# 42 instead of 68 early unit matrix matmuls, and narrow matmuls first in three of seven products

## The chip, the core and the metric

The kernel runs on one core of a Trainium2 chip. A core has a matmul engine (TensorE, PE in the profile, with its weight loads as PEld), VectorE (DVE), ScalarE (ACT), GpSimd (POOL) and SyncE (SP), which here issues DMAs. The metric is the device time of one execution in microseconds, as a median over several executions.

## What is computed

One layer of a hybrid encoder: the input, 512 tokens of width 2048 in float32, is normalised and projected by one large matrix. Its columns give four matrices (q, k, v and a gate) for each of three branches of four heads, and three merge gates of width 2048. Each branch is an attention of its own kind; the outputs are gated, projected up, weighted by the merge gates, summed, projected once more and added to the input.

```python
hn = rmsnorm(x, norm_g)
proj = jnp.einsum('bsd,dc->bsc', hn, w_in)
...
ya = forgetting_attention(qa, ka, to_heads(br[:, :, 0, 2]), f_logit)
yb = chunked_relpos_attention(qb, kb, to_heads(br[:, :, 1, 2]), rel_bias)
yc = stick_breaking_attention(to_heads(br[:, :, 2, 0]), to_heads(br[:, :, 2, 1]), to_heads(br[:, :, 2, 2]))
ys = jnp.stack([from_heads(ya), from_heads(yb), from_heads(yc)], axis=2)
ys = ys * jax.nn.silu(br[:, :, :, 3])
up = jnp.einsum('bsnw,nwd->bsnd', ys, w_up)
merged = jnp.sum(gates * up, axis=2)
return x + jnp.einsum('bsd,de->bse', merged, w_out)
```

## The kernel before

**Split numbers.** Every float32 operand is split into an upper part, rounded to a reduced float32 that TensorE multiplies in one pass, and a lower part, the rest (`split`, lines 242 to 251: ScalarE writes the upper part at L245, VectorE the lower at L249). A product is then upper x upper + upper x lower + lower x upper.

**Stages.** At the start TensorE runs `WARM` matmuls of a 128x128 unit matrix in bfloat16 (L403). Their result is never read. Then come:

- the first head: q, k, v and gate of branch C, head 0, side by side, as x arrives (`first_quad`; units 0 to 8). TensorE also multiplies by the forget gate's few columns (L1174), and a small matmul (L479) spreads the row norms, copied by ScalarE to `rstd` (L484). VectorE then scales the sixteen tiles of x (L500) and they are split again (L245, L249);
- four gate columns on the whole of x (`col_task`), units 9 to 16, in 512-column matmuls;
- from then on input columns by pairs, with Strassen's scheme in Winograd's form (`PairTask`): seven products instead of eight. There are 52 pairs: a gate pair beside the first head, three pairs for head (C,1), four for each of nine heads, four for the last head, (A,3), and at the very end, after the up projection, eight of the output projection.

**A unit.** A pair has seven units, one for each product p. A unit takes eight tiles j of 128x128 weights, as upper part `u.hi` and lower part `u.lo` (in the profile `wh` and `wl`, 128x1024 each). On each tile's upper part TensorE runs a matmul of 512 columns (upper and lower part of the input, side by side: the two halves of the bank), and on each tile's lower part one of 256 columns, onto the left half. All eight wide ones come first, then the eight narrow ones. The order of the products is (1, 2, 6, 5, 7, 3, 4), except in pairs called `late`. Products 6, 7 and 4 are summed onto the bank in which 1, and then 6 and 7, already lie (`more`), and 3 onto that of 5. Each waits for the copy of the bank's earlier sum (`self.ev[onto]`), and between the two stands a unit of another bank.

**Weights of a unit.** `prep` splits them two units ahead (`LA = 2`): three buffers of `wh` and of `wl` rotate. The lower part is awaited by `yield u.ready`, which stands between wide and narrow matmuls.

**The order of work.** A planner (`Flow`) runs while the program is written: it simulates TensorE, ScalarE and VectorE with fixed costs, and the order in which it starts instructions is the order in which they stand on each engine. Attention matmuls (scores, transposes, products with v) are slipped in between a unit's matmuls as they become ready. The unit matrix matmuls are no part of the plan.

Of the kernel before, what the change touches and what calls it, by code (L numbers as in the profile page):

```python
# [16 lines left out]
S = 512  # L17
D = 2048
HD = 128
NH = 4  # L20
# [5 lines left out]
UK = 8  # L26
NQ = 4
HS = S // 2
EPS = 1e-6
NEG = -1e30  # L30
WARM = 68
SCALE = HD ** -0.5
LA = 2

A, B, C = 0, 1, 2
Q, K, V, G = 0, 1, 2, 3
PE, ACT, DVE = 0, 1, 2
# [112 lines left out]
def mm_us(n, x=1):  # L150
    return x * max(0.115, n / 2400 + 0.0133)
# [11 lines left out]
def hybrid_kernel(  # L163
# [26 lines left out]
    def nm(s):  # L190
        uid[0] += 1
        return f"{s}_{uid[0]}"
# [12 lines left out]
    def acc(i=0):  # L205

        return pa.tile([P, S], F32, tag=f"acc{i}", name=nm("acc"), bufs=1 if i else 2)
# [10 lines left out]
    LH, RH = slice(0, HS), slice(HS, S)  # L218

    def two(ap):  # L220

        return ap.rearrange("p (h s) -> p h s", h=2)

    class Parts:


        def __init__(self, s, ev=None):
            self.t = xp.tile([P, 2, 2, HS], F32R, tag="x", name=nm(s))
            self.hi, self.lo = self.t[:, :, 0, :], self.t[:, :, 1, :]
            self.ev = ev or [Event(), Event()]  # L230
# [32 lines left out]
    def mm(ps, w, x, start=False, stop=False, more=False):  # L263
        nc.tensor.matmul(ps, w, x, start=start, stop=stop, skip_group_check=more)  # L264
# [70 lines left out]
    units = []  # L335
# [65 lines left out]
    nc.vector.memset(first_ps, 0.0)  # L401
    for _ in range(WARM):
        nc.tensor.matmul(first_ps[:, :P], identb, identb, start=True, stop=True)  # L403
# [137 lines left out]
    def strassen_ops(x1, x2, t23, t4):  # L541

        def part(ts, i):
            return lambda k: ts[k] and ts[k].both(i)

        return {1: part(x1, 0), 2: part(x2, 0), 3: part(x2, 1), 5: part(x1, 1), 6: part(t23, 0), 7: part(t23, 1),
                4: lambda k: t4[k // 2] and t4[k // 2].both(k % 2)}


    def halves(c):  # L550
        return [w_col[c, 0], w_col[c, 1]]
# [50 lines left out]
    class PairTask:  # L602
# [6 lines left out]

        def __init__(self, src1, src2, ops, c1_done=None, c2r_done=None, c2_done=None, late=False, rest=None):
            self.src, self.ops, self.late, self.rest = (*src1, *src2), ops, late, rest
            self.done = {"c1": c1_done, "c2r": c2r_done, "c2": c2_done}
            self.order = (1, 5, 2, 3, 6, 7, 4) if late else (1, 2, 6, 5, 7, 3, 4)
            self.w, self.there, self.ps = {}, {p: Event() for p in range(1, 8)}, {}
            self.ev = {p: Event() for p in range(1, 8)}
            self.units = [Pair(self, i) for i in range(7)]
# [36 lines left out]
        def mms_of(self, i):  # L655
            p = self.order[i]
            bank = (0, 1, 2, 0, 0, 1, 2)[i] if self.late else {2: 1, 5: 2, 3: 2}.get(p, 0)
            onto = None if self.late else {6: 1, 7: 6, 4: 7, 3: 5}.get(p)
            more = onto is not None
            self.bank = getattr(self, "bank", {})  # L660
            self.bank[p] = bank

            def go(u):
                if more:
                    yield self.ev[onto]
                    self.ps[p] = self.ps[onto]
                else:
                    yield accs[bank], 1
                    self.ps[p] = acc(bank)

                for j in range(UK):
                    yield lambda: self.ops[p](j) is not None
                    r, _, ev = self.ops[p](j)
                    yield ev
                    yield PE, mm_us(S)
                    mm(two(self.ps[p]), u.hi[:, j, :], r, j == 0 and not more, more=more)
                yield u.ready
                for j in range(UK):
                    yield PE, mm_us(HS)
                    mm(self.ps[p][:, LH], u.lo[:, j, :], self.ops[p](j)[1], stop=j == UK - 1, more=more)  # L680
            return go

        def after_of(self, i):
# [434 lines left out]
    def col(n, r, h):  # L1118
        return halves((n * 4 + r) * NH + h)

    def gate_col(n, d):
        return halves(NB * 4 * NH + n * DT + d)

    ops = strassen_ops(x1, x2, t23, t4)
    gates = [(n, d) for n in range(NB) for d in range(0, DT, 2)]

    def spill(n, d, c):
        gl[n, d] = dp.tile([P, S], F32, name=nm("gl"))
        nc.sync.dma_start(gl[n, d], c)
        stored(t2s, 1, 256)  # L1130

    def gate_units(late=False):
        n, d = gates.pop(0)

        def keep(i):
            def go(c):
                spill(n, d + i, c)
                return
                yield
            return go  # L1140
        units.extend(PairTask(gate_col(n, d), gate_col(n, d + 1), ops, keep(0), None, keep(1), late).units)

    def first_quad(head):

        ps = {}
# [79 lines left out]
    def schedule(head, a, b):  # L1225
        for (d, g), base in [(g, a) for g in head.stages()[0]] + [(g, b) for g in head.stages()[1]]:
            at(base + d, g)

    def first_head(n, h):
        hd = Head(n, h)  # L1230
        units.extend(first_quad(hd))

        cols = []
        for _ in range(2):
            g, d = gates.pop(0)
            cols += [(g, d), (g, d + 1)]
        t = [col_task(gate_col(*c), spilled(*c), b, used_g if i == 3 else None)
             for i, (c, b) in enumerate(zip(cols, (1, 2, 0, 0)))]
        for i in range(2):
            units.extend(u[i] for u in t)  # L1240
        at(OFF["fb"], forget_bias)
        gate_units(late=True)
        schedule(hd, OFF["a0"], OFF["b0"])

    def head(n, h, last=False):
        hd = Head(n, h, last)
        u0 = len(units)
        units.extend(PairTask(col(n, Q, h), col(n, K, h), ops, hd.got(Q), None, hd.got(K)).units)
        if not last and (n, h) != (C, 1):
            gate_units()  # L1250
        units.extend(PairTask(col(n, V, h), col(n, G, h), ops, hd.got(V), None, hd.got(G)).units)
        gate_units()
        if last:
            gate_units()
        schedule(hd, u0 + 7, u0 + 21)
        return hd

    first_head(C, 0)
    for n, h in [(C, 1), (C, 2), (C, 3)] + [(n, h) for n in (B, A) for h in range(NH)]:
        last_head = head(n, h, (n, h) == (A, NH - 1))  # L1260


# [307 lines left out]
```

## Time and profile before

| | us |
|---|---|
| median of 3 runs | 1339.41 |
| lowest and highest | 1338.91, 1339.82 |
| profiled execution, its own time | 1340.63 |
| span of that execution, first to last instruction | 1338.9 |
| TensorE busy in the span | 1324.5 |
| VectorE busy | 1113.1 |
| ScalarE busy | 793.0 |

A row of a timeline gives the start, the time to the end of the last of its instructions, the engine, the line of the kernel, the operation, what is written and read by the program's names, the shape and the count; in brackets stands the engine's idle time before it and what ended it. Ends of matmuls are modelled, so their pace is read from starts. A row of waits names the waiting engine and line, what it waited for, the sum, the number and the longest. A row of stretches gives the stretch, its length, busy time and count of the engine's instructions, the granted clock of TensorE, the share of DMA time and GB/s; a count includes instructions that run over the stretch's edge.

### The profile page before, as it was taken

What the parts mean: (1) busy time and instruction counts of PE and PEld (TensorE: products, weight loads), DVE (VectorE), ACT (ScalarE), POOL (GpSimd) and SP (SyncE); (2) the same over time, 40 slices, a digit from 0 to 9 for tenths busy, and PEclk for the clock granted to TensorE, in tenths of its full rate; (3) what the DMA queues carried; (4) which work ended last, traced back from release to release, by engine and by line L of the source; (5) the groups of instructions that cost most, each with busy time, mean ns of one, the idle gap of its engine ahead of it and who ended that gap; (6) DMA issues with size and microseconds to landing.
All of it is one profiled execution on the core that took longest, in us unless ns stands there. A gap on an engine that the chain in (4) does not pass through costs nothing.

```text
span 1338.9 us, 19796 instructions
## 1 busy us (share of the span) xinstructions
PE 1324.5 (99%) x7390; PEld 1148.3 (86%) x7390; DVE 1113.1 (83%) x1626; ACT 793.0 (59%) x1215; POOL 91.6 (7%) x115
## 2 busy tenths in 40 slices
PE   9999999999999999999999999999999999989998
PEld 7788888888888888888888888888888788878887
DVE  5899998888787887878888888878788877897786
ACT  7656665646566566665666556665577655444443
POOL 0000101000010000010000001000000000001000
PEclk9999999999999999999999999999999999989999
DMA  9457767677767777677877768777768655758883
GB/s 359 166 137 182 182 178 184 193 196 200 198 176 201 187 216 180 182 204 174 226 179 190 192 181 215 176 189 200 196 184 267 234 189 188 197 142 244 240 244 90
DMA packets 89824, 263.06 MB, mean 196 GB/s; under 512 B 10480, under 2 KB 12656, under 8 KB 89728
## 3 DMA queue, kind: packets, MB, share of 16 engines
q1 hardware_dynamic: 71152, 203.00, 45.5%
q0 software_dynamic: 14976, 54.53, 24.7%
q10 hardware_dynamic: 3600, 4.26, 0.9%
q8 instruction: 58, 0.95, 0.3%
q14 instruction: 38, 0.31, 0.1%
HBM read 242.06 MB, written 19.70 MB: 196 GB/s over the span
## 4 chain that ended last, share of the span: by engine, by line
PE 98%; DVE 1%; POOL 0%; issue 0%; ACT 0%; DVEq 0%; ACTq 0%; POOLq 0%
PE acc L264 84%; PE att L264 8%; PE att L986 1%; PE att L1090 1%; PE att L1089 1%; PE att L260 1%; PE att L261 1%; PE att L259 1%; PE att L1088 1%; PE att L403 0%; DVE wl L249 0%; PE att L1049 0%; PE att L1174 0%; PE att L890 0%; PE att L889 0%; DVE m L249 0%
## 5 line engine op out<-in xcount | busy, mean ns | idle before, releaser
L249 DVE TENSOR_TENSOR wl<-raw,wh 128x1024 fp32r<-128x1024 f32 (+2 forms) x413 | 493.9, 1196 | 145.2 <-ACT wh L245 141.8
L245 ACT ACTIVATE wh<-raw 128x1024 fp32r<-128x1024 f32 (+2 forms) x413 | 427.7, 1037 | 145.3 <-PE acc L264 62.8
L264 PE MATMUL acc<-x,wh 128*128 128x512 f32 x1600 | 415.4, 395 | 0.0
L264 PEld LDWEIGHTS acc<-x,wh 128*128 128x128 f32 x1600 | 285.8, 189 | 52.4 <-ACT x L245 2.6
L264 PE MATMUL acc<-t,wh 128*128 128x512 f32 x1056 | 271.7, 394 | 0.0
L264 PEld LDWEIGHTS acc<-x,wl 128*128 128x128 f32 x1504 | 210.4, 190 | 18.5 <-issue 0.5
L264 PE MATMUL acc<-x,wl 128*128 128x256 f32 (+1 forms) x1504 | 223.6, 289 | 0.0
L264 PEld LDWEIGHTS acc<-t,wh 128*128 128x128 f32 x1056 | 188.0, 189 | 32.1
L264 PEld LDWEIGHTS acc<-t,wl 128*128 128x128 f32 x1056 | 145.4, 190 | 11.1
L264 PE MATMUL acc<-t,wl 128*128 128x256 f32 x1056 | 149.2, 282 | 0.0
L280 POOL DMA_DIRECT2D raw<-in_w_col x88 | 76.1, 865 | 927.0 <-DMA raw<-in_w_col 572.5
L264 PE MATMUL acc<-m,wh 128*128 128x512 f32 x448 | 113.9, 396 | 6.3 <-DVE m L249 5.9
L264 PEld LDWEIGHTS acc<-m,wh 128*128 128x128 f32 x448 | 81.6, 191 | 21.6 <-DVE m L249 6.3
L756 ACT ACTIVATE c<-acc 128x256 f32<-128x256 f32 x50 | 19.1, 383 | 98.8 <-PE acc L264 93.8
L734 ACT ACTIVATE u<-acc 128x512 f32<-128x512 f32 x50 | 29.8, 596 | 64.9 <-PE acc L264 64.9
L264 PE MATMUL att<-y,wh 128*128 128x512 f32 x256 | 66.5, 390 | 1.3 <-DVE y L249 1.3
L264 PEld LDWEIGHTS acc<-m,wl 128*128 128x128 f32 x448 | 61.9, 193 | 5.1 <-DVE wl L249 0.8
L264 PE MATMUL acc<-m,wl 128*128 128x256 f32 x448 | 63.3, 285 | 0.4 <-DVE wl L249 0.4
L646 DVE TENSOR_TENSOR raw<-raw,raw 128x1024 f32<-128x1024 f32 x52 | 63.4, 1219 | 0.4
L640 DVE TENSOR_TENSOR raw<-raw,raw 128x1024 f32<-128x1024 f32 x52 | 63.4, 1218 | 0.4
L717 ACT ACTIVATE v<-acc 128x512 f32<-128x512 f32 x52 | 31.2, 599 | 50.3 <-PE acc L264 47.0
L264 PEld LDWEIGHTS att<-y,wh 128*128 128x128 f32 x256 | 47.9, 188 | 12.3 <-DVE y L249 2.4
(183 smaller groups left out, 1362.4 us busy)
## 6 DMA issues: line engine op xcount, KB each, us to landing
raw<-in_w_col SPq DMA_DIRECT2D x228, 512.0 KB, 4.5
raw<-in_w_col POOLq DMA_DIRECT2D x88, 512.0 KB, 6.4
raw<-in_w_out SPq DMA_DIRECT2D x40, 512.0 KB, 4.4
gl<-c SPq DMA_DIRECT2D x48, 256.0 KB, 2.7
raw<-in_w_up SPq DMA_DIRECT2D x32, 384.0 KB, 3.1
sg<-gl SPq DMA_DIRECT2D x48, 256.0 KB, 5.1
raw<-in_w_out POOLq DMA_DIRECT2D x16, 512.0 KB, 6.5
x<-in_xT SPq DMA_DIRECT2D x16, 256.0 KB, 6.1
```

Of the source, the lines that this page charges most:

```text
L245: nc.scalar.activation(hi, src, AF.Copy)
L249: nc.vector.tensor_sub(lo, src, f(hi))
L259: nc.tensor.matmul(ps, lh, rh, start=start, stop=False, skip_group_check=more)
L260: nc.tensor.matmul(ps, lh, rl, start=False, stop=False, skip_group_check=more)
L261: nc.tensor.matmul(ps, ll, rh, start=False, stop=stop, skip_group_check=more)
L264: nc.tensor.matmul(ps, w, x, start=start, stop=stop, skip_group_check=more)
L280: nc.gpsimd.dma_start(to, src, accum_op=ALU.add)
L640: nc.vector.tensor_add(w[1], w[1], w[5])
L646: nc.vector.tensor_add(w[2], w[2], w[1])
L717: nc.scalar.activation(self.v, ps, AF.Copy)
L734: nc.scalar.activation(self.u, ps, AF.Copy)
L756: nc.scalar.activation(c, ps[:, RH], AF.Copy, scale=-1.0)
```

## The change

`WARM` becomes 42. A flag `turns` is handed to the pairs; where it is set, products 6, 7 and 4 run their eight narrow matmuls first and the eight wide ones then. The flag is set for all pairs of the nine heads between (C,1) and (A,3), their gate pairs included: 36 pairs. The pairs of (C,1) and (A,3), the late ones and the output projection keep their order.

```diff
-WARM = 68
+WARM = 42
...
-                for j in range(UK):
-                    yield lambda: self.ops[p](j) is not None
-                    r, _, ev = self.ops[p](j)
-                    yield ev
-                    yield PE, mm_us(S)
-                    mm(two(self.ps[p]), u.hi[:, j, :], r, j == 0 and not more, more=more)
-                yield u.ready
-                for j in range(UK):
-                    yield PE, mm_us(HS)
-                    mm(self.ps[p][:, LH], u.lo[:, j, :], self.ops[p](j)[1], stop=j == UK - 1, more=more)
+                def wide(last):
+                    for j in range(UK):
+                        yield lambda: self.ops[p](j) is not None
+                        r, _, ev = self.ops[p](j)
+                        yield ev
+                        yield PE, mm_us(S)
+                        mm(two(self.ps[p]), u.hi[:, j, :], r, j == 0 and not more, last and j == UK - 1, more=more)
+
+                def narrow(last):
+                    yield u.ready
+                    for j in range(UK):
+                        yield lambda: self.ops[p](j) is not None
+                        _, r, ev = self.ops[p](j)
+                        yield ev
+                        yield PE, mm_us(HS)
+                        mm(self.ps[p][:, LH], u.lo[:, j, :], r, stop=last and j == UK - 1, more=more)
+                for step, last in ((narrow, False), (wide, True)) if p in (6, 7, 4) and self.turns else (
+                        (wide, False), (narrow, True)):
+                    yield from step(last)
...
     for n, h in [(C, 1), (C, 2), (C, 3)] + [(n, h) for n in (B, A) for h in range(NH)]:
+        turning[0] = (n, h) not in ((C, 1), (A, NH - 1))
         last_head = head(n, h, (n, h) == (A, NH - 1))
```

More of the change, by code (lines that the diff above doesn't have):

```diff
@@ L602, in hybrid_kernel, with __init__ @@
     class PairTask:
-        def __init__(self, src1, src2, ops, c1_done=None, c2r_done=None, c2_done=None, late=False, rest=None):
-            self.src, self.ops, self.late, self.rest = (*src1, *src2), ops, late, rest
+        def __init__(self, src1, src2, ops, c1_done=None, c2r_done=None, c2_done=None, late=False, rest=None, turns=False):
+            self.src, self.ops, self.late, self.rest, self.turns = (*src1, *src2), ops, late, rest, turns
             self.done = {"c1": c1_done, "c2r": c2r_done, "c2": c2_done}
@@ L1125, in hybrid_kernel @@
     gates = [(n, d) for n in range(NB) for d in range(0, DT, 2)]
+    turning = [False]
     def spill(n, d, c):
@@ L1140, in keep @@
             return go
-        units.extend(PairTask(gate_col(n, d), gate_col(n, d + 1), ops, keep(0), None, keep(1), late).units)
+        units.extend(PairTask(gate_col(n, d), gate_col(n, d + 1), ops, keep(0), None, keep(1), late,
+                              turns=turning[0]).units)
     def first_quad(head):
@@ L1247, in head @@
         u0 = len(units)
-        units.extend(PairTask(col(n, Q, h), col(n, K, h), ops, hd.got(Q), None, hd.got(K)).units)
+        units.extend(PairTask(col(n, Q, h), col(n, K, h), ops, hd.got(Q), None, hd.got(K), turns=turning[0]).units)
         if not last and (n, h) != (C, 1):
             gate_units()
-        units.extend(PairTask(col(n, V, h), col(n, G, h), ops, hd.got(V), None, hd.got(G)).units)
+        units.extend(PairTask(col(n, V, h), col(n, G, h), ops, hd.got(V), None, hd.got(G), turns=turning[0]).units)
         gate_units()
```

## The prediction

> **What bounds the kernel now.** I read the page's busy times, its chain of work, the waits of TensorE, and then TensorE's stretches.
>
> ```profile
> PE 1324.5 (99%) x7390; PEld 1148.3 (86%) x7390; DVE 1113.1 (83%) x1626; ACT 793.0 (59%) x1215; POOL 91.6 (7%) x115
> PE 98%; DVE 1%; POOL 0%; issue 0%; ACT 0%; DVEq 0%; ACTq 0%; POOLq 0%
> PE acc L264 <- DVE m L249: 5.9, 1, 5.9
> 58.00:1040.00 982.00, 982.00 (x5643) 1.00 0.72 191
> ```
>
> TensorE is busy 99% of the span, and the chain of waits is 98% TensorE. Its one large wait (5.9 us, third row) lies at the start of the output projection, which the change does not reorder. The last row is a stretch of 982 us: TensorE never stands idle in it, at full clock. All 36 reordered input pairs lie there. So time can be won in two ways only: start the dense stream earlier, or let the same matmuls follow each other more closely. It is lost if something new makes TensorE wait.
>
> **Part one: 26 fewer unit matrix matmuls.** The rows are the start of TensorE and of ScalarE, then TensorE's matmul counts in stretches.
>
> ```profile
> 2.12 6.48 PE L403 MATMUL att<-identb 128*128 128x128 bf16 x68 [2.12 <-DVE identb L312]
> 8.41 0.70 PE L264 MATMUL acc<-x,wh 128*128 128x512 f32 x2
> 4.58 0.72 ACT L419 ACTIVATE x<-x,small_in 128x512 fp32r<-128x512 f32 x1 [2.50 <-DMA x<-in_xT]
> 5.21 0.61 ACT L245 ACTIVATE wh<-raw 128x512 fp32r<-128x512 f32 x1
> 3.00:4.00 1.00, 1.00 (x12) 1.00 1.05 387
> 3.00:7.00 4.00, 4.00 (x41) 1.00 1.03 374
> 7.60:7.80 0.20, 0.20 (x7) 1.00 1.06 410
> 7.60:8.30 0.70, 0.70 (x16) 1.00 1.04 395
> ```
>
> The operands of the first real matmul are there at 5.21 + 0.61 = 5.82 us, yet it starts at 8.41, behind the 68 unit matmuls. Between 4 and 7 us there are 41 - 12 = 29 starts, about 105 ns each; between 7.8 and 8.3 us there are 9, or 55.6 ns. So the array runs at half pace first, and the pace doubles on the way. 68 matmuls in 8.41 - 2.12 = 6.29 us, n of them at 107 ns and the rest at 55.6, give n = 49: the change of pace is near 7.35 us. With 42, real work begins at 2.12 + 42 x 0.107 = 6.6 us, after the operands. If the pace still changes at 7.35, the first 0.75 us of real work does half of what it would do later, so its start is worth 6.6 + 0.37 = 6.97 us, 1.44 us earlier. That is 26 x 55.6 ns: wherever the change of pace falls between 6.6 and 8.4, the matmuls taken away are worth their fast price. The upper bound, with no slow start of the real ones, is 8.41 - 6.6 = 1.8 us; the lower is nothing, if what follows is late.
>
> What follows is the first stage, and there the nearest operand is the lower part of x tile 7 in the first gate column. The rows are of TensorE, ScalarE and VectorE.
>
> ```profile
> 37.24 1.02 PE L479 MATMUL att<-dg,tmpc 128*128 128x512 f32 x2
> 36.75 0.61 ACT L245 ACTIVATE x<-x 128x512 fp32r<-128x512 f32 x1
> 38.30 0.60 ACT L484 ACTIVATE rstd<-att 128x512 f32<-128x512 f32 x1 [0.93 <-PE att L479]
> 38.93 1.29 DVE L500 TENSOR_TENSOR x<-x,rstd 128x512 f32<-128x512 f32 x2 [0.22 <-ACT rstd L484]
> 40.49 1.22 DVE L249 TENSOR_TENSOR wl<-raw,wh 128x1024 fp32r<-128x1024 f32 x1 [0.26 <-ACT wh L245]
> 46.31 1.23 DVE L249 TENSOR_TENSOR wl<-raw,wh 128x1024 fp32r<-128x1024 f32 x1 [0.24 <-ACT wh L245]
> 57.65 3.94 PE L264 MATMUL acc<-x,wh 128*128 128x512 f32 x16
> 59.94 1.28 DVE L249 TENSOR_TENSOR x<-x,x 128x512 fp32r<-128x512 f32 x2
> ```
>
> TensorE takes two wide matmuls for each x tile from 57.65 on. The sixteenth, which reads x tile 7's lower part, starts at 61.2 us: the sixteen last 3.94 us, one alone 0.4 (its end is modelled), so the sixteenth starts 3.94 - 0.4 = 3.54 after the first. VectorE writes that part in the first half of the last row, done near 60.6: TensorE has 0.6 us of slack, and would want this tile 1.44 us earlier. VectorE is without a gap from 46.31 to that row, so it comes earlier only by the gaps ahead of it: 0.22, 0.26 and 0.24 us. These close, because ScalarE's copy of rstd waits 0.93 us for the matmul at 37.24; with TensorE earlier it starts when ScalarE is free, at 36.75 + 0.61 = 37.36. VectorE is then 0.72 us earlier, and TensorE can be 0.6 + 0.72 = 1.3 us earlier. I take 1.25; bounds 0.6 (no gap closes) and 1.44.
>
> **Part two: narrow matmuls first in products 6, 7 and 4.** No matmul, load, DMA or evacuation is added or removed; only the order within a unit turns. The order of a pair was, with W for eight 512-column matmuls and N for eight 256-column ones: 1 WN, 2 WN, 6 WN, 5 WN, 7 WN, 3 WN, 4 WN. It becomes 1 WN, 2 WN, 6 NW, 5 WN, 7 NW, 3 WN, 4 NW. Going round from 4 to the next 1, N is followed by W 7 times before and 4 times after, so each pair loses 3 steps of each kind. The question is what a step costs. The rows are TensorE's, of the gate columns, of undisturbed pair units, and of one place with a longer run of short matmuls.
>
> ```profile
> 63.24 3.79 PE L264 MATMUL acc<-x,wh 128*128 128x512 f32 x16
> 79.56 0.62 PE L264 MATMUL acc<-x,wh 128*128 128x512 f32 x2
> 125.56 2.00 PE L264 MATMUL acc<-x,wh 128*128 128x512 f32 x8
> 127.41 1.11 PE L264 MATMUL acc<-x,wl 128*128 128x256 f32 x8
> 147.91 0.40 PE L264 MATMUL acc<-t,wh 128*128 128x512 f32 x1
> 508.58 0.40 PE L264 MATMUL acc<-x,wl 128*128 128x256 f32 x2
> 509.06 2.00 PE L264 MATMUL acc<-t,wh 128*128 128x512 f32 x8
> 1025.72 0.29 PE L1088 MATMUL att<-ah,vh 128*128 128x256 f32 x1
> 1027.38 2.00 PE L264 MATMUL acc<-t,wh 128*128 128x512 f32 x8
> 1029.22 1.11 PE L264 MATMUL acc<-t,wl 128*128 128x256 f32 x8
> ```
>
> Wide matmuls among themselves: 63.24 to 79.56 is three gate units of 24, so 16.32 / 72 = 0.2267 us each, 1.813 for eight. Narrow ones among themselves: the fifth of a unit starts at 508.58, the next unit at 509.06, so 0.48 / 4 = 0.120 us each, 0.960 for eight. A unit would be 2.773 us. But eight whole units from 125.56 to 147.91 take 22.35, that is 2.794 each: a pair of steps costs 0.02 us. (The first W there takes 127.41 - 125.56 = 1.85: the cost sits in the wide matmuls after narrow ones.) It goes away only if sixteen narrow ones leave no more behind them than eight. The last three rows speak for that: six short matmuls and then a unit's eight narrow ones, 14 in all, run before 1027.38, and the wide eight after them take 1.84, as everywhere. So I count 3 x 36 x 0.0204 = 2.2 us. Bounds: 2.2, and a loss of 0.8, if the wide ones pay by the number of narrow ones before them and only the quicker start of N after W goes (some 7 ns, 108 times).
>
> The cover that goes: a turned unit needs its lower weights at its first matmul, where it had 1.84 us of wide ones in front. Each unit has one such row, so they are counted off against TensorE's; VectorE's row stands before the unit that it feeds.
>
> ```profile
> 504.88 1.22 DVE L249 TENSOR_TENSOR wl<-raw,wh 128x1024 fp32r<-128x1024 f32 x1
> 510.40 1.21 DVE L249 TENSOR_TENSOR wl<-raw,wh 128x1024 fp32r<-128x1024 f32 x1
> 515.10 0.86 PE L264 MATMUL acc<-t,wh 128*128 128x512 f32 x3
> 190.40 1.19 DVE L249 TENSOR_TENSOR wl<-raw,wh 128x1024 fp32r<-128x1024 f32 x1
> 192.39 2.00 PE L264 MATMUL acc<-t,wh 128*128 128x512 f32 x8
> 196.65 1.21 DVE L249 TENSOR_TENSOR wl<-raw,wh 128x1024 fp32r<-128x1024 f32 x1
> 197.98 2.00 PE L264 MATMUL acc<-t,wh 128*128 128x512 f32 x8
> ```
>
> Product 6 at 509.06 has its weights at 506.10, and product 7 at 515.10 at 511.61: 3.0 and 3.5 us to spare. The tightest place is the first turned pair, where stick-breaking scans fill VectorE: 0.8 us at 192.39 and 197.98 - 197.86 = 0.1 at product 7. With TensorE earlier there, some tenths may be waited. What waits is TensorE itself, and all matmuls behind it. The upper weights' buffer is also held 0.95 us longer, to the end of a turned unit; the order by hand places the split that reuses it after that end anyway. The bank waits do not change, since a whole unit lies between a product and the one added onto it. I take 0.2 us for new waits, bounds 0 and 1.
>
> Sum: -1.25 - 2.2 + 0.2 = -3.25 us. The profiled execution took 1340.63 us (span 1338.9), so 1337.4; the median of the runs is 1339.41, 1.2 lower, and there the sum gives **1336.2**.
>
> **The rivals.**
>
> (a) *The order is worth nothing.* Only the early start stays: -1.25, or 1338.2. The Trainium skill, "TensorE: Matmul & The Clock Gate", section "Back-to-back issue gap", gives the warm gap as N / 2.4 ns plus 2.5, with no word of the matmul before it, and by it turning the order would move nothing. Against it: 1.84 to 1.85 us for eight wide ones after narrow ones, 1.813 among wide ones. For it: a longer narrow run is shown at one place only.
>
> (b) *The early start is mostly used up.* TensorE arrives at x tile 7 and waits for VectorE, whose gaps do not close: 0.6 instead of 1.25, and a few tenths more in the first turned pair, so -2.2 - 0.6 + 0.3 = -2.5, or 1336.9. For it: VectorE's gapless rows from 46 to 60 us.
>
> (c) *Slower: turned units wait for their lower weights.* The place is the first matmul of each of 108 units, the price what VectorE is late. It decides from 3.45 / 108 = 32 ns a unit on; for a loss that can be told (0.2%, 2.7 us, is about what a measurement of this kernel tells from no change) it takes 57 ns, 6.2 us in all, or 1342.2. For it: VectorE is 83% busy, with 0.1 us to spare at 197.98. Against it: 3 us to spare elsewhere, so ten or more heads' worth of such places would be needed.
>
> (d) *It does not do what it says.* The flag is set ahead of each head and handed to its four pairs, so 9 x 4 = 36 pairs turn; products 3, added too, do not. I see no way past that, and give it no chance.
>
> **Chances and range.** The row is TensorE's, around the wait of 5.9 us.
>
> ```profile
> 1180.00:1188.00 8.00, 2.13 (x9) 0.81 0.60 145
> ```
>
> The granted clock is 0.81 on the mean there, so half for some 3 us. How long it stays low may change with where the wait falls in time; I allow 1 us either way. Forecast 0.58 (1335.2 to 1336.7 as its own range, that included), (a) 0.20, (b) 0.14, (c) 0.08. Faster by over 0.2% means below 1336.7: the forecast, 0.58. Within 0.2%: (a) and (b), 0.34. Slower: 0.08. The range reaches over the forecast, (b) and (a) with half a microsecond around them: 1334.8 to 1338.8.
>
> **What would show it.** The first real matmul near 6.6 us, and at 57.65 the same row about 1.3 us earlier; a step of TensorE's waits for VectorE's x near 59.5 us if (b). Runs of sixteen narrow and sixteen wide matmuls in the turned pairs: W16 near 16 x 0.2267 + 0.03 = 3.66 us if right, near 3.69 if the order is worth nothing. New rows "PE acc <- DVE wl" among the waits of TensorE would speak for (c). Wrong would be the whole if the 982 us stretch had idle time, or if the wait of 5.9 us grew as the work before it came earlier.

## The result

| | median, us | lowest and highest | executions |
|---|---|---|---|
| before | 1339.71 | 1338.89, 1341.13 | 20 |
| changed | 1337.01 | 1335.86, 1337.99 | 20 |

The ratio is 0.9977 (95% interval 0.9971 to 0.9983): 3.1 us less by the ratio, between 2.3 and 3.9; by the medians 2.7. The forecast was 3.25 us less and 1336.2 us. The profiled execution of the changed kernel took 1337.21 us (span 1335.5), 3.4 under the one of before.

The busy times on the page of the changed kernel:

```profile
PE 1321.0 (99%) x7364; PEld 1148.0 (86%) x7364; DVE 1112.6 (83%) x1626; ACT 791.0 (59%) x1215; POOL 91.7 (7%) x115
```

Two rows of its waits of TensorE (us in all, count, longest):

```profile
PE acc L264 <- DVE m L249: 5.9, 1, 5.9
PE acc L264 <- DVE wl L249: 0.4, 1, 0.4
```

TensorE in the stretch that answers to 58 to 1040 us of before (window, its length, busy time and count, granted clock, DMA share, GB/s):

```profile
56.60:1036.40 979.80, 979.80 (x5643) 1.00 0.72 192
```

The same 5643 matmuls, still without idle time, take 2.2 us less than 982.0. The wait of 5.9 us is as long as before, and the wait for `wl` is the one near the end that was there before. No new wait of the narrow matmuls shows among the waits. The start, in TensorE's timeline and then in VectorE's:

```profile
2.13 4.66 PE L403 MATMUL att<-identb 128*128 128x128 bf16 x42 [2.13 <-DVE identb L312]
6.55 1.15 PE L264 MATMUL acc<-x,wh 128*128 128x512 f32 x2
7.54 0.63 PE L264 MATMUL att<-x,wh 128*128 128x512 f32 x2
56.23 3.94 PE L264 MATMUL acc<-x,wh 128*128 128x512 f32 x16
```

```profile
59.18 1.29 DVE L249 TENSOR_TENSOR x<-x,x 128x512 fp32r<-128x512 f32 x2
```

Real work begins 1.86 us earlier, but its first two matmuls take 0.99 us instead of 0.54: they run at half clock. (The column for the granted clock reads 1.00 in such early rows too; the trace's record of it begins with its first change, to full, at 7.52 us here and at 7.43 in the profile of before. I say that the clock opens at that moment; ahead of it the pace shows the half clock.) At the first gate column 1.42 us of it are left (57.65 to 56.23), and the row of VectorE that the prediction took for x tile 7 comes 0.76 us earlier. Last, undisturbed turned units and the tightest place, in TensorE's timeline:

```profile
639.32 1.11 PE L264 MATMUL acc<-x,wl 128*128 128x256 f32 x8
640.27 1.12 PE L264 MATMUL acc<-t,wl 128*128 128x256 f32 x8
641.24 2.00 PE L264 MATMUL acc<-t,wh 128*128 128x512 f32 x8
643.08 1.98 PE L264 MATMUL acc<-x,wh 128*128 128x512 f32 x8
644.89 1.11 PE L264 MATMUL acc<-x,wl 128*128 128x256 f32 x8
...
195.59 1.11 PE L264 MATMUL acc<-x,wl 128*128 128x256 f32 x8
196.59 1.19 PE L264 MATMUL acc<-t,wl 128*128 128x256 f32 x8
197.62 1.33 PE L264 MATMUL acc<-t,wh 128*128 128x512 f32 x5
```

Sixteen narrow ones take 641.24 - 639.32 = 1.92 us, and the sixteen wide ones behind them 644.89 - 641.24 = 3.65: eight at 1.84, the next eight at 1.81. The extra time is paid once for a run of sixteen. At the tightest place, two runs of eight narrow ones take 197.62 - 195.59 = 2.03 instead of some 1.91: 0.12 us waited for the lower weights.

### The profile page after: what moved, and what is told of

It is laid out like the page before. It is cut to its first block, busy times and chain, and to the rows that moved or that the text cites. A ratio compares the mean times of both kernels' runs of the same rounds, so it can differ in the third digit from the quotient of the medians.

```text
span 1335.5 us, 19770 instructions
## 1 busy us (share of the span) xinstructions
PE 1321.0 (99%) x7364; PEld 1148.0 (86%) x7364; DVE 1112.6 (83%) x1626; ACT 791.0 (59%) x1215; POOL 91.7 (7%) x115
## 4 chain that ended last, share of the span: by engine, by line
PE 98%; DVE 1%; POOL 0%; issue 0%; ACT 0%; DVEq 0%; ACTq 0%; POOLq 0%
PE acc L264 84%; PE att L264 8%; PE att L995 1%; PE att L1098 1%; PE att L1099 1%; PE att L260 1%; PE att L261 1%; PE att L259 1%; PE att L1097 1%; DVE wl L249 0%; PE att L1058 0%; PE att L403 0%; PE att L1185 0%; PE att L899 0%; PE att L898 0%; DVE m L249 0%
## 5 line engine op out<-in xcount | busy, mean ns | idle before, releaser
L264 PEld LDWEIGHTS acc<-x,wh 128*128 128x128 f32 x1600 | 292.8, 188 | 58.9 <-ACT x L433 0.9
L264 PE MATMUL acc<-t,wh 128*128 128x512 f32 x1056 | 268.6, 393 | 0.0
L264 PE MATMUL acc<-t,wl 128*128 128x256 f32 x1056 | 152.7, 284 | 0.0
L264 PEld LDWEIGHTS acc<-t,wl 128*128 128x128 f32 x1056 | 139.6, 191 | 2.2
```

## The experiments

In each table, the starts of TensorE are those of the first real matmul, of the first matmul of 256 columns (the first pair), and of the first matmul of the up projection. The part between the last two holds all turned pairs; I call what a kernel saves in it the gain of the stream. Starts are those of each kernel's one profiled execution; leads are counted against the profile of before.

### One part alone

Two kernels: before with `WARM = 42`, and the change with `WARM = 68`.

```diff
-WARM = 68
+WARM = 42
```

> The kernel before with 42 unit matrix matmuls, order of the products as before. My theory, each matmul taken away is worth its fast price: 26 x 55.6 ns = 1.4 us faster. Rival, VectorE's tile 7 swallows half of it: 0.6 us faster. The two parts together measured 2.7 us; if they only add, the other part has the rest.

```diff
-WARM = 42
+WARM = 68
```

> The change with 68 unit matrix matmuls: the turned order alone. My theory, 108 steps from narrow to wide at 0.02 us: 2.1 us faster, the first real matmul at 8.4 us as before. Rival, the order is worth nothing: 0, and the whole change would be the early start. Sixteen wide matmuls in a row would then take 3.68 us and not 3.66.

| | median, us | ratio to before, interval | first real | first pair | up projection | lead at first pair | gain of the stream |
|---|---|---|---|---|---|---|---|
| before | | | 8.41 | 103.13 | 1038.50 | | |
| change | 1337.01 | 0.9977 (0.9971 to 0.9983) | 6.55 | 101.72 | 1034.99 | 1.41 | 2.10 |
| 42 alone | 1339.55 | 0.9996 (0.9987 to 1.0005) | 5.82 | 101.71 | 1037.09 | 1.42 | -0.01 |
| order alone | 1337.85 | 0.9983 (0.9974 to 0.9992) | 8.10 | 102.84 | 1036.11 | 0.29 | 2.10 |

The order alone is faster and gains 2.10 us in the stream, as in the change: rival (a) falls, and the two parts do not need each other. In the two profiles of the change and of before, 1.41 at the start and 2.10 in the stream, less 0.1 behind the late wait, make the whole difference of 3.4 us. The lead of 0.29 us of the order alone is none of its own: its clock opened earlier in that execution, at 6.77 us instead of 7.43.

The 42 alone cannot be told from no change by the times: its median is 0.56 us under that of the kernel before beside it (1340.11), near the rival's 0.6, and the interval of the ratio, from 1.7 us faster to 0.7 slower, leaves room for the theory's 1.4 as well. Its profile says why the lead is less than it could be. Here are TensorE at the start, TensorE further on, and ScalarE there:

```profile
3.70 2.31 PE L403 MATMUL att<-identb 128*128 128x128 bf16 x27
5.82 0.72 PE L264 MATMUL acc<-x,wh 128*128 128x512 f32 x2
```

```profile
34.27 0.61 PE L264 MATMUL att<-x,wl 128*128 128x512 f32 x2
35.74 1.10 PE L479 MATMUL att<-dg,tmpc 128*128 128x512 f32 x2 [0.86 <-ACT dg L475]
```

```profile
33.37 1.06 ACT L245 ACTIVATE wh<-raw 128x1024 fp32r<-128x1024 f32 x1 [1.40 <-DMA raw<-in_w_first]
34.34 1.26 ACT L475 ACTIVATE dg<-identf,small_n 128x128 f32<-128x128 f32 x4
```

In this execution the clock opened early, at 5.03 us, the unit matmuls were done at 5.8 us and the first real ones ran at once at full pace: 2.6 us ahead of the profile of before. At 35 us TensorE waits 0.86 us for the copies `dg`, which feed the norms' matmul (L479). They stand behind the split of unit 6's weights on ScalarE, and that waits 1.40 us for its DMA. Behind it 1.42 us of lead are left. The change has as much, but not for this reason. In its profile TensorE shows no wait at that place (ScalarE's row of the copies, then TensorE's):

```profile
34.29 1.27 ACT L475 ACTIVATE dg<-identf,small_n 128x128 f32<-128x128 f32 x4
35.83 1.02 PE L479 MATMUL att<-dg,tmpc 128*128 128x512 f32 x2
```

The copies end at 35.56 us, 0.27 before the matmul starts; where TensorE waits, it is some 0.15 (35.60 to 35.74 above). The change's lead is 1.41 from its third real matmul on: that is what its late clock left of it. So this matmul caps a lead that would be larger, and x tile 7, which I had named, does not. The cap is no fixed 1.4 us: it moves with the copies, and below it leaves 1.56 and 1.68 us in two other profiles.

### Other numbers of steps

The change with product 3 turned as well, and before with every unit of the 36 pairs in four runs of four.

```diff
-                for step, last in ((narrow, False), (wide, True)) if p in (6, 7, 4) and self.turns else (
+                for step, last in ((narrow, False), (wide, True)) if p in (6, 7, 4, 3) and self.turns else (
```

> The change with product 3 turned too: more turned units, but only 2 steps fewer in a pair than in the kernel before (5 of 7 stay), not 3. My theory, time follows the steps: 36 x 0.02 = 0.7 us slower than the change, so 2.0 us faster than the kernel before. Rival, each turned unit brings the gain for itself (its weights or its bank come better): 36 more of them are 0.7 us faster than the change, 3.4 us faster than before.

```diff
+                a, b = range(UK // 2), range(UK // 2, UK)
+                if self.turns:
+                    for step, js, last in ((wide, a, False), (narrow, a, False), (wide, b, False), (narrow, b, True)):
+                        yield from step(last, js)
+                else:
+                    yield from wide(False)
+                    yield from narrow(True)
```

> The kernel before, with four wide, four narrow, four wide, four narrow matmuls in every unit of the 36 pairs: 252 steps from narrow to wide more. My theory, each step has its price whatever the length of the narrow run: about 252 x 0.02 = 5 us slower, at least 4, since a run of four ends before the fifth slow wide matmul. Rival, the wide ones pay by the number of narrow ones before them: no change. Rival, order is worth nothing: no change.

| | median, us | ratio to before, interval | first pair | up projection | gain of the stream |
|---|---|---|---|---|---|
| four products turned | 1337.51 | 0.9979 (0.9970 to 0.9988) | 101.45 | 1035.04 | 1.78 |
| runs of four | 1342.41 | 1.0018 (1.0009 to 1.0027) | 102.91 | 1040.22 | -1.94 |

More turned units gain less (1.78 against 2.10), so the gain is no gift to each turned unit; by steps it should have been 1.4 to 1.5. Counted in the traces, attention matmuls included, a 512-column matmul follows a shorter one 409 times before, 276 times in the change and 295 times here. By that count the gains stand in the same proportion: 2.10 us for 133 steps fewer, 1.78 for 114, 16 ns each. That the attention matmuls, which fall into other places, bring the difference is therefore likely; no run tests it. Splitting a unit loses time, which neither rival allows, but 1.9 us and not 4 to 5. Its timeline of TensorE, two undisturbed units:

```profile
623.25 1.09 PE L264 MATMUL acc<-t,wh 128*128 128x512 f32 x4
624.18 0.63 PE L264 MATMUL acc<-t,wl 128*128 128x256 f32 x4
624.65 1.09 PE L264 MATMUL acc<-t,wh 128*128 128x512 f32 x4
625.58 0.64 PE L264 MATMUL acc<-t,wl 128*128 128x256 f32 x4
626.06 1.09 PE L264 MATMUL acc<-x,wh 128*128 128x512 f32 x4
```

A unit takes 2.81 us (623.25 to 626.06) against 2.79 of before. Four wide ones take 0.93 where 0.907 is their price among themselves: each run pays nearly the whole extra. But the narrow runs are shorter too, 0.47 and 0.48, so a second step in a unit costs some 0.013 us net, not 0.020. That would be 3.3 us for 252 units; where the other 1.4 went I did not settle. The count in the trace, 643 steps and so 234 more than before, does not account for it.

### The wait of 5.9 us and the clock

The times of one kernel spread over some 2 us, nearly as much as the effect. TensorE's row for 1184 to 1192 us, just behind the wait, in the profile of before:

```profile
1184.00:1192.00 8.00, 4.81 (x16) 0.57 0.86 198
```

The granted clock is 0.57 of full there. In each of the eight profiles without filling the wait is 5.9 us, and the half clock lasts 6.83 us; but only 3.0 (order alone) to 5.9 us (runs of four) of it fall on work, the rest on the wait. So 100 unit matmuls, never read, were put into the wait, in the kernel before and in the changed one:

```diff
+                        if self.rest is not None and self.late and p == 6 and j == UK - 1:
+                            yield atts, 1
+                            ps = att()
+                            for _ in range(FILL):
+                                nc.tensor.matmul(ps[:, :P], identb, identb, start=True, stop=True)
+                            give(atts)
                         yield ev
                         yield PE, mm_us(S)
```

> The kernel before, with 100 unit matrix matmuls (never read) put where TensorE waits 5.9 us at the start of the output projection, in product 6 of the first output pair, ahead of its last wide matmul. They fill 5.6 us of that wait. My theory: the spread of the kernel's times (1338.8 to 1341.1) is mostly the half clock after this wait, whose length (3.0 to 5.9 us in the profiles so far) hangs on the phase of the clock's windows; with the wait filled the half clock does not come, the median falls by about 2.0 us to 1338 and the granted clock shows no 0.5 near 1185 us. Rival, the clock has no part in it: the same time, or up to 0.5 us slower where a filled matmul delays the first real one.

> The changed kernel with the same 100 matmuls in the same wait. My theory: 1335.0 us median with a spread under 1 us, so 2.9 to 3.1 us under the filled kernel before: with one of the two sources of spread gone, the change shows its stream gain of 2.1 us and an early start of 0.8 to 1.0 us. Rival, the early start is worth 1.4 us in every execution: 3.5 us under the filled kernel before. Rival, it is worth nothing on the mean: 2.1 us under it.

Later the two parts were run alone with this filling.

> The kernel before with the late wait filled (that alone: 1338.2 us) and with 42 unit matrix matmuls; the order of the products as before. My theory, an early start of 1.4 us in executions whose clock opens late and less where it opens early, since TensorE then meets the norms' matmul: 0.8 to 1.0 us under the filled kernel before on the median, 1337.3, and a spread of about 0.5 us instead of 1.6. Rival, 26 x 55.6 ns in every execution: 1.4 us, 1336.7, and the same spread.

> The kernel before with the late wait filled and the turned order, 68 unit matrix matmuls. My theory, 2.1 us under the filled kernel before in every execution: 1336.1, with its spread of about 1.6 us. Rival, the order's gain depends on the early start: less than 1.5 us.

| wait filled | median, us | lowest and highest | executions | ratio to the kernel before, interval |
|---|---|---|---|---|
| before | 1338.16 | 1337.28, 1338.85 | 11 | 0.9989 (0.9981 to 0.9998) |
| 42 alone | 1336.93 | 1336.74, 1337.38 | 11 | 0.9978 (0.9969 to 0.9987) |
| order alone | 1335.87 | 1335.33, 1336.40 | 7 | 0.9971 (0.9960 to 0.9981) |
| change | 1335.14 | 1334.84, 1335.32 | 5 | 0.9967 (0.9955 to 0.9980) |

TensorE in the filled kernel before, the same eight microseconds:

```profile
1184.00:1192.00 8.00, 7.74 (x86) 1.00 0.86 214
```

The half clock is gone, the median falls by 1.4 to 1.5 us (2.0 were expected), and the spread of before by 0.7 us, from 2.2 to 1.6; that of the change falls from 2.1 to 0.5, in five executions. So the clock behind the wait made part of the spread, and of the kernel before not the larger part, as the theory had it. What is left of it in the filled kernel before, 1.6 us, goes with the start: with 42 unit matmuls it shrinks to 0.6. The profiles, ordered by the moment at which the clock opens, show how:

| unit matmuls | profile of | clock opens, us | lead at first pair, us |
|---|---|---|---|
| 68 | wait filled, before | 8.13 | -0.36 |
| 68 | before | 7.43 | 0 |
| 68 | runs of four | 6.93 | 0.22 |
| 68 | order alone | 6.77 | 0.29 |
| 68 | wait filled, order alone | 5.91 | 0.69 |
| 42 | wait filled, 42 alone | 7.80 | 1.26 |
| 42 | change | 7.52 | 1.41 |
| 42 | four products turned | 6.72 | 1.68 |
| 42 | wait filled, change | 5.28 | 1.56 |
| 42 | 42 alone | 5.03 | 1.42 |

With 68, the lead grows by nearly half of what the clock opens earlier, over a range of 1.05 us. With 42 it grows as well down to 6.72 us and is smaller for the two that open earlier still: they have more at first (2.5 and 2.6 us) and lose it to operands. That is the cap at work, and it has a second place, which took 0.5 us from the filled change, a wait for a part of x:

```profile
12.81 0.73 PE L265 MATMUL acc<-x,wh 128*128 128x512 f32 x2 [0.24 <-ACT x L246]
```

The change is worth 3.0 us between filled kernels, the order 2.3, and 42 for 68 between 0.7 (with the order turned) and 1.2 (without, where the theory had 0.8 to 1.0 and the rival 1.4). The order alone spreads over 1.1 us, not 1.6. These differences cross two sets of executions on different occasions, and by the ratios each has an interval of more than 1 us; the medians fit the account of the profiles and do not prove it.

### Fewer unit matmuls still

The change with `WARM = 16`.

```diff
-WARM = 42
+WARM = 16
```

> The changed kernel with 16 unit matrix matmuls; they end near 3.9 us, and TensorE stands idle until the first operands at 5.8 us. Theory, the clock opens only after a window of about 3.4 us that is mostly busy, so the idle time puts the opening off: real matmuls at half pace until 8 to 11 us, and about 1 us slower than the change, though the first real matmul is earlier. Rival, only the place of the first real matmul counts: the same as the change, since it already runs into the wait for the norms' matmul, or faster by up to 0.5 us.

It took 1337.70 us (ratio to before 0.9985, interval 0.9976 to 0.9994), 0.7 over the change, which the intervals do not tell apart. Its timeline of TensorE does:

```profile
2.12 1.89 PE L403 MATMUL att<-identb 128*128 128x128 bf16 x16 [2.12 <-DVE identb L312]
5.83 1.22 PE L264 MATMUL acc<-x,wh 128*128 128x512 f32 x2 [1.82 <-ACT wh L245]
8.55 1.06 PE L264 MATMUL att<-x,wh 128*128 128x512 f32 x2
9.40 1.06 PE L264 MATMUL acc<-x,wl 128*128 128x512 f32 x2
10.26 0.79 PE L264 MATMUL att<-x,wl 128*128 128x512 f32 x2
10.89 0.62 PE L264 MATMUL acc<-x,wh 128*128 128x512 f32 x2
```

Real work begins at 5.83 as it should, and runs two matmuls in 0.85 us (8.55 to 9.40), half pace, until after 10.3 us; the record has full clock from 10.62 on. At the first pair (102.81) only 0.32 us of the lead of 2.58 are left. In none of the thirteen other profiles does the clock open later than 8.13 us, so the idle 1.82 us put its opening off; this is one execution.

### Lifting the cap

ScalarE's copies for the norms' matmul go ahead of the weights of unit 6 (the edit holds back units 6 to 8), alone, with the wait filled, and with 35 unit matmuls besides.

```diff
         yield u.source_there()
+        if u in units[6:9]:
+            yield dg_ev
         yield from split(u.hi, u.lo, u.source(), n, u.ready, hi_ev=u.ready_hi)
...
             nc.scalar.activation(dg[:, blk(b)], identf, AF.Copy, scale=y[:, b:b + 1])
+        set_(dg_ev)
```

> The changed kernel with ScalarE's order turned at one place: the four copies that feed the norms' small matmul go ahead of the split of the weights of unit 6, which waits for its DMA. Theory, what caps the early start is that matmul (in the run with 42 unit matmuls alone TensorE waited 0.9 us for it and gave back 1.1 us of a 2.5 us lead): the wait of TensorE for ScalarE's copies goes, executions whose clock opens early keep their lead, and the median falls by 0.3 to 0.5 us against the change. Rival, the lower part of x tile 7 caps it just as well: no change, and TensorE then waits for VectorE near 59 us.

> The changed kernel with the late wait filled (that alone: 1335.1 us, spread 0.5) and ScalarE's copies for the norms' matmul put ahead of the weights of unit 6. My theory, the cap of the early start was that matmul: the lowest times fall to about 1333.8, the median by 0.4 to 0.8 us, and the spread grows to over 1 us. Rival, x tile 7 caps it just as well: the same median and spread.

> As the one before, with 35 unit matrix matmuls, which end near 5.9 us, when the first operands are there. Theory, without the cap each matmul taken away is worth up to 55.6 ns: 7 of them 0.3 to 0.4 us. Rival, something else in the first stage caps: no change against the one before.

| | median, us | lowest and highest | executions | ratio to before, interval |
|---|---|---|---|---|
| copies first | 1336.87 | 1335.87, 1338.53 | 11 | 0.9980 (0.9971 to 0.9989) |
| wait filled, copies first | 1334.95 | 1334.56, 1335.42 | 5 | 0.9964 (0.9951 to 0.9976) |
| the same with 35 | 1334.48 | 1334.29, 1334.73 | 5 | 0.9960 (0.9947 to 0.9972) |

The first two are inconclusive: 0.1 and 0.2 us under the kernels without it, less than the theories' 0.3 to 0.8, and the profiled executions of both had a late clock (7.79 and 7.99 us), so that no cap was met. In the third the clock opened at 6.97 us. This is its timeline, of TensorE and then of ScalarE (the edits shift the line numbers: L483 here is L479 of the kernel before):

```profile
34.28 1.02 PE L483 MATMUL att<-dg,tmpc 128*128 128x512 f32 x2
37.46 0.61 PE L265 MATMUL att<-x,wh 128*128 128x512 f32 x2
38.05 0.73 PE L265 MATMUL acc<-x,wh 128*128 128x512 f32 x2
```

```profile
35.93 1.06 ACT L246 ACTIVATE wh<-raw 128x1024 fp32r<-128x1024 f32 x1 [1.31 <-DMA raw<-in_w_first]
36.90 0.58 ACT L488 ACTIVATE rstd<-att 128x512 f32<-128x512 f32 x1
37.38 0.62 ACT L246 ACTIVATE x<-x 128x512 fp32r<-128x512 f32 x1
```

The norms' matmul starts at 34.28 without a wait (it stands four matmuls earlier in TensorE's order here), and the lead of 2.0 us is the same ahead of it and behind it. The next thing caps: at 38.05 TensorE is late by some tenths (0.59 us between two starts instead of 0.45), for a part of x that ScalarE writes from 37.38 on, behind a split that waited 1.31 us for its DMA. 1.75 us of lead are left at the first pair (101.38), against 1.68 at most with the copies in their old place. With the first stage's loads as they are, another cap follows closely. This version, 1334.48 us, is the fastest of all, 5.4 us under the kernel before by the ratio.

The same profile settles x tile 7. TensorE at the end of the first gate unit, then VectorE:

```profile
59.22 0.62 PE L265 MATMUL acc<-x,wh 128*128 128x512 f32 x2
59.67 0.62 PE L265 MATMUL acc<-x,wl 128*128 128x512 f32 x2
59.30 1.28 DVE L250 TENSOR_TENSOR x<-x,x 128x512 fp32r<-128x512 f32 x2
```

All sixteen wide matmuls have started before 59.67 us, without a wait, while the first half of VectorE's row ends only after 59.9. So that row does not write what they read.

## The prediction, step by step

- **What bounds it.** Right. The stretch has no idle time after the change either, and the gain came from an earlier start and a closer sequence. The wait of 5.9 us stayed 5.9. The half clock behind it was misread: "half for some 3 us" is what the row from 1180 to 1188 us holds, and it goes on to 1191.9, 6.83 us in all. No term of the sum hangs on it, only the 1 us either way in the range.
- **26 unit matmuls at their fast price, 1.44 us.** Right for an execution whose clock opens as late as in the profile of before: 1.41 at the first pair, with the two real matmuls at half pace that the sum allowed for. That the clock of the changed kernel's profile opened at nearly the same moment (7.52 against 7.43 us) is luck; in the other profiles it opens anywhere from 5.0 to 8.1, or 10.6 with 16 unit matmuls.
- **The cap, 1.25 us.** The working is wrong, and that the profile shows 1.41 is luck: it is the 1.44 of the term above, with no cap met. I named x tile 7. VectorE's gaps closed as I said (0.76 us instead of 0.72), but the row at 59.94 that I took for the tile writes others (the profile with 35 shows it). Counted in order, it holds tiles 8 and 9, which TensorE reads from unit 13 on, and tile 7 is the row at 55.81, done 4.7 us before its matmul: nothing was near there. What caps the lead, where the clock opens early, is the norms' matmul, whose row I had quoted: I read it only as what releases VectorE, not as a wait of TensorE itself, and did not set its operand's end against it. And the profile is one draw: where the clock opens early, the kernel before has part of the lead already and the change gains less. Over many executions the early start was worth 0.7 to 1.2 us, by the filled kernels.
- **108 steps at 0.02 us, 2.2 us, less 0.2 for new waits.** Right: 2.10 in the stream, in the change and alone, with 0.12 us waited at the place that was named, product 7 near 196 us. In the traces a unit's wide matmul stands directly behind a narrow one 108 times less, and 2.10 + 0.12 us over 108 is 0.0206 us a step. Wide runs of sixteen took 3.65, as forecast for a price that does not grow with the narrow run. That the price is fixed for any length is not so: with runs of four a further step cost about two thirds in undisturbed units, and less on the whole.
- **(a)** falls by the order alone and by the runs of four. The Trainium skill's formula in "TensorE: Matmul & The Clock Gate", section "Back-to-back issue gap", knows nothing of the matmul before; here the same matmuls in another order took 2.10 us less, and the measurement decides.
- **(b)** was nearer in time than the forecast: the median, 1337.01 us, lies 0.1 from its 1336.9, and outside the forecast's own range (1335.2 to 1336.7). By the difference, the 2.7 us of the medians are nearer to its 2.5 than to the forecast's 3.25, the 3.1 of the ratio nearer to the forecast. Its mechanism, a wait at x tile 7, was not there; an early start used up by an operand was seen in a run, at another instruction.
- **(c)** had its price once, 0.12 us, instead of 108 times.

The shortfall of the median against the forecast is 0.8 us in time and 0.55 in difference: 0.3 of the 0.8 is the kernel before, whose median is 1339.71 here and was 1339.41 ahead of the prediction. The 3.25 us lie within the interval of the ratio. The early start, which hangs on the clock's phase, is the term that the runs make smaller.

## What to carry to other kernels

Where a profile is one execution and a clock's phase differs between executions, ask of each microsecond won at the start whether every execution has it to win, and look for the first operand that arrives on a time of its own: a fixed arrival turns an earlier start into a wait. A row that releases another engine is also an instruction with operands of its own; set them against it. In a dense stream of matmuls the order of two widths is worth reading from the starts, and merging runs cost next to nothing here, 0.12 us at one place, since the operands mostly lay ready far ahead.

## What the runs showed of the hardware

- Eight matmuls of 512 columns behind narrower ones take 1.84 us instead of 1.81, and the extra lies in the first five (234, 236, 228, 232 and 231 ns from start to start behind the sixteen narrow ones, then 227); sixteen narrow ones before them make it no larger (3.65 us for sixteen). Why the width ahead matters, no run here shows.
- With an idle stretch of 1.82 us early on, full clock came at 10.6 us; in the thirteen other profiles it came between 5.0 and 8.1. The Trainium skill, "TensorE: Matmul & The Clock Gate", section "Part 1: The HAM clock gate (the "warmup" mystery)", says that a free-running window of about 3.4 us decides; the shift by about 3 us, the changing moment of opening (with the same 42 unit matmuls 5.03 us in one profile and 7.80 in another) and the half clock of 6.83 us behind the late wait, two such windows, agree with it.
- 100 matmuls that nobody reads, in a wait that the kernel leaves empty, made the kernel 1.5 us faster by the ratio (0.9989); the clock behind the wait stayed at 1.00 instead of 0.57.
